# An encoder's residual, added by a DMA from GpSimd instead of a load and a VectorE addition

## The chip, the cores and the metric

The kernel runs on one core of a Trainium2 chip. The core has five engines that run side by side, each in its own fixed order of instructions: TensorE (PE, with its weight loads as PEld), VectorE (DVE), ScalarE (ACT), GpSimd (POOL) and SyncE (SP). They meet through semaphores: an instruction waits until another engine, or a DMA, has counted up. DMAs are started by an instruction on SP, ACT or POOL and then run on the core's 16 DMA engines.

The metric is the device time of one execution in microseconds (us), median over runs. Three runs of the kernel before took 2087.84, 2090.29 and 2091.57 us, so the median is 2090.29 us.

## The reference

A two-layer encoder over one sequence of 1024 tokens of width 1024, all in float32. Each layer is

```python
h = _rmsnorm(x, g_pre_mix[l])
z = h @ w_in[l]                       # split in Fourier, q, k, v and memory-query parts
y_f = _fourier_mix(zf, w_fourier[l])
y_a = _window_attn(q, k, v, sink[l])  # 8 query heads, window of 128
y_m = _memory_attn(zm, km, vm)
y = concat([_rmsnorm(y_f), _rmsnorm(y_a), _rmsnorm(y_m)]) @ w_out[l]
x = x + _rmsnorm(y, g_post_mix[l])    # the addition that the change moves

h = _rmsnorm(x, g_pre_ffn[l])
gate, up = split(h @ w_ffn_in[l])
f = (silu(gate) * up) @ w_ffn_out[l]
x = x + _rmsnorm(f, g_post_ffn[l])
```

with `_rmsnorm(y, g) = y * rsqrt(mean(y*y) + 1e-6) * g` over a row of 1024.

## The kernel before

**Tiles.** The 1024 tokens are 8 tiles (t = 0 to 7) of 128 partitions x 1024 floats. Float32 products are made from two float32r halves of each operand (`split`, L151 on ACT and L152 on DVE or POOL), three matmuls per product.

**The stage around the change.** Of the product with w_out, the Fourier and memory groups come first; their sum goes to DRAM (`pmd`). Then a loop over i (L1383 ff.) is skewed over the tiles: it does the attention of the second key/value head for tile i (`att_units`, scores sc, softmax scaling by POOL at L785, transposes pT, values av), the attention group's product with w_out for tile i-2 (`out`, matmuls `mo`), and the transposes of the finished rows of tile i-4 into the FFN's operand blocks (`Blocks.tile`, matmuls `hTp`, L1066). `Blocks.sum` and `Blocks.last` then form the sums and halves that the FFN's block products (a Strassen scheme, matmuls qx, qy, qz, qw, L1137) need.

**One tile's rows.** `out_rows` loads two tiles of rows by SP: f, the partial sum from `pmd` (L1027), and x, the residual from the input or, in the second layer, from the first layer's result `x2d` (L1028). `out` adds the matmul result to f (two DVE instructions at L1041). `residual` squares f with a row sum on ACT (L335), takes the reciprocal root on POOL (two instructions of one column, L210 and L212, names rrsv and rrs), scales f on DVE (L337) and adds it to x on DVE (L338). `norm_x` squares x on ACT (L289), stores x to `x1d` by an ACT DMA (L291), takes the root on POOL (nrsv, nrs) and scales x into f's place on DVE (L294). What lies in f then is the FFN's input, which PE transposes. The scale grs of the attention group is a POOL instruction too (L962), after the DVE instruction ms (L960).

**Places in SBUF.** x and f come from a ring of six places of 4 KB per partition (`xfs`, numbers 16, 20, 24, 28, 32, 0): tile 5 has x in 32 and f in 0, tile 6 has x in 16 and f in 20, tile 7 has 24 and 28. The first four weight loads of the FFN (two for the gate quad, two for the up quad, L1112) go to 32, 0, 16 and 20, so they wait until tiles 5 and 6 have left them.

**What sets the order.** The program is written as a list of operations, and a scheduler with its own model of times fixes the order on each engine, PE and SP included; at run time each engine keeps that order. A DVE addition that becomes a DMA is therefore also a cause for another order.

Of the kernel before, what the change touches and what calls it, by code (L numbers as in the profile page):

```python
# [16 lines left out]
ALU = mybir.AluOpType  # L17
# [3 lines left out]
D = 1024  # L21
S = 1024
NT = S // P
# [43 lines left out]

@with_exitstack
def tile_encoder(ctx: ExitStack, tc: tile.TileContext, T, C, out):
    nc = tc.nc  # L70

# [49 lines left out]
    def run(k, n, step):  # L121
        return Ring(*[k + i * step for i in range(n)])
# [6 lines left out]
    sqs, pms, xfs = run(16, 2, 2), run(20, 2, 2), Ring(16, 20, 24, 28, 32, 0)  # L129
# [8 lines left out]
    def sm(n, name="v"):  # L138
        if name not in smp:
            smp[name] = ctx.enter_context(tc.tile_pool(name="sm_" + name, bufs=N_SM.get(name, 4)))  # L140
        return smp[name].tile([P, n], F32, tag=name, name=nm(name))

    def ps(shape, name="ps", tag="pd"):
        return psp[tag].tile([P] + list(shape), F32, tag=tag, name=nm(name))
# [24 lines left out]
    def cst(*shape):  # L169
# [20 lines left out]
        out=mask[:, 0:P], in_=mask[:, 0:P], pattern=[[1, P]], compare_op=ALU.is_ge,  # L190
# [4 lines left out]
        out=mask[:, 2 * P : 3 * P], in_=mask[:, 2 * P : 3 * P], pattern=[[-1, P]],  # L195
# [11 lines left out]
    def rsqrt_mean(ss, n, width, name="rs"):  # L207

        v = sm(width, name + "v")
        nc.gpsimd.tensor_scalar(out=v, in0=ss, scalar1=1.0 / n, scalar2=EPS, op0=ALU.mult, op1=ALU.add)  # L210
        r = sm(width, name)
        nc.gpsimd.tensor_tensor(out=r, in0=v, in1=mhalf[:, 0:width], op=ALU.pow)  # L212
        return r
# [72 lines left out]
    def norm_x(x, g, h=None, keep=None):  # L286

        ss = sm(1, "nss")
        nc.scalar.activation(junks(D // 2).bitcast(BF16) if h is None else h, x, AF.Square, accum_out=ss)  # L289
        if keep is not None:  # L290
            nc.scalar.dma_start(keep, x)  # L291
        h = x if h is None else h
        r = rsqrt_mean(ss, D, 1, "nrs")
        nc.vector.scalar_tensor_tensor(out=h, in0=x, scalar=r[:, 0:1], in1=g, op0=ALU.mult, op1=ALU.mult)  # L294
        return h
# [32 lines left out]
            (nc.gpsimd if t in (1, 3) else nc.vector).tensor_tensor(out=x[:, ns], in0=x[:, ns], in1=f[:, ns], op=ALU.add)  # L328
            (nc.sync, nc.scalar)[n].dma_start(dst[:, ns], x[:, ns])

    def residual(x, f, g, eng=None):

        junk = junks(D // 2).bitcast(BF16)
        ss = sm(1, "rss")
        nc.scalar.activation(junk, f, AF.Square, accum_out=ss)  # L335
        r = rsqrt_mean(ss, D, 1, "rrs")
        nc.vector.scalar_tensor_tensor(out=f, in0=f, scalar=r[:, 0:1], in1=g, op0=ALU.mult, op1=ALU.mult)  # L337
        (eng or nc.vector).tensor_tensor(out=x, in0=x, in1=f, op=ALU.add)  # L338


    def scaled(raw, g, k):
# [144 lines left out]
    class Mix:  # L486
# [536 lines left out]
            self.prepped[t] = self.split_y(parts, yys), self.group_scale(parts, AW, sqs)  # L1023

        def out_rows(self, t, xsrc, pmd):
            self.xf[t] = x, f = xfs(D), xfs(D)
            nc.sync.dma_start(f, pmd)  # L1027
            nc.sync.dma_start(x, xsrc)  # L1028

        def out(self, t, x1):  # L1030

            x, f = self.xf.pop(t)
            (hi, lo), rs = self.prepped.pop(t)
            for n in range(2):
                ns = slice(n * 512, n * 512 + 512)
                pt = ps([512], "mo")
                acc = Acc(pt, 4)
                for i in range(4):
                    w = self.woa[2 + i]
                    acc.add(hi[:, i], lo[:, i], w[0][:, ns], w[1][:, ns])  # L1040
                nc.vector.scalar_tensor_tensor(  # L1041
                    out=f[:, ns], in0=pt, scalar=rs[:, 0:1], in1=f[:, ns], op0=ALU.mult, op1=ALU.add
                )
            residual(x, f, self.gpost)
            return norm_x(x, self.gffn, f, x1)


# [181 lines left out]
    def out_sums(l, actd, i, k):  # L1229
# [23 lines left out]
        return ab  # L1253

    def ffn_out(l, actd, load, out, after, half, late):


# [14 lines left out]
        for i in (5, 3, 4, 1, 7, 2, 6):  # L1272
# [5 lines left out]
            for k in range(n):  # L1278
                ops.append(out_sums(l, actd, i, k))
                for p in range(whole):  # L1280
                    step(pts[p], p, ops[k], k == 0, k == n - 1, new)
                t = {(2, 2): 0, (2, 7): 1, (6, 1): 2, (6, 5): 3}.get((i, k))
                if t is not None:
                    load(t)
                    out(t, rows[t])
                if i == 6 and k in (7, 8, 9, 10):
                    load(k - 3)
# [71 lines left out]
    for l in range(DEPTH):  # L1359
# [69 lines left out]
        def last_tile(t, f):  # L1429
            if t == 0:  # L1430
                st["gpf"] = gain(T["g_post_ffn"][l], at(8, D))
            x = xt.pop(t)
            if l == DEPTH - 1:
                residual_out(x, f, st["gpf"], x_out[t], t)
                return
            residual(x, f, st["gpf"], nc.gpsimd if t < 4 else None)
            nc.sync.dma_start(x2d[t], x)
            token_scale(x, t)
            st[t] = x
            if t:  # L1440
                norm_T(st.pop(t - 1), nhT, t - 1, "av")
# [62 lines left out]
```

## Time and profile before

| | |
|---|---|
| median of three runs (range) | 2090.29 us (2087.84 to 2091.57) |
| the profiled execution: span from its first to its last instruction | 2089.2 us |
| mean granted TensorE clock in it | 0.981 |
| PE busy | 1994.7 us (95%) |
| DVE busy | 1578.8 us (76%) |
| ACT busy | 1069.9 us (51%) |
| POOL busy | 713.1 us (34%) |

The page lists the span of the profiled execution and no separate time for it; the span lies 1.1 us under the median of the runs. The stage of the change runs from about 320 to 424 us in layer 0 and from about 1350 to 1450 us in layer 1. In the rows of a timeline the columns are start, duration, engine, line, operation, written tile<-read tiles, shape and count; in brackets the idle time before it and what ended that. In a table of windows each engine's column is its busy time with its count of instructions.

### The profile page before, as it was taken

How to read it: one execution, taken by the hardware profiler on the slowest of the kernel's cores; microseconds unless marked ns; L12 is line 12 of the kernel's file. 1: busy time of each engine (PE TensorE's matmuls, PEld its weight loads, DVE VectorE, ACT ScalarE, POOL GpSimd, SP SyncE). 2: the span in 40 equal slices, each digit the busy share in tenths (PEclk: the TensorE clock that was granted, in tenths of full speed). 3: DMA queues.
4: the chain of work that ended last, by engine and by line, in shares of the span. 5: the costliest groups of instructions: out<-in, count | busy, mean ns of one | idle time of the engine just before them, and what ended most of it. 6: DMA issues, size and time to landing. Idle time of an engine off the chain costs nothing.

```text
span 2089.2 us, 28535 instructions
## 1 busy us (share of the span) xinstructions
PE 1994.7 (95%) x9587; PEld 1646.5 (79%) x9587; DVE 1578.8 (76%) x2540; ACT 1069.9 (51%) x2270; POOL 713.1 (34%) x819
## 2 busy tenths in 40 slices
PE   7998999799999999999999979997999999989998
PEld 6876787578888888887788768775788888878886
DVE  5558767898787877778867686579878787778767
ACT  6467777654333333544555677675433333345441
POOL 4344435433333423002523544453343342320002
PEclk9999999999999999999999999998999999999999
DMA  6111132423232333879831122233233232269874
GB/s 211 51 51 61 56 112 91 162 71 101 97 120 87 126 96 116 312 271 328 279 133 45 48 66 86 77 134 118 86 104 114 86 131 96 92 210 343 303 261 151
DMA packets 173347, 286.48 MB, mean 137 GB/s; under 512 B 15464, under 2 KB 73360, under 8 KB 173200
## 3 DMA queue, kind: packets, MB, share of 16 engines
q1 hardware_dynamic: 165136, 265.78, 37.9%
q10 hardware_dynamic: 8064, 18.88, 2.3%
q8 instruction: 75, 1.23, 0.2%
q14 instruction: 72, 0.59, 0.1%
HBM read 218.02 MB, written 66.58 MB: 136 GB/s over the span
## 4 chain that ended last, share of the span: by engine, by line
PE 74%; DVE 9%; DMA 7%; ACT 5%; issue 3%; POOL 2%; SPq 0%; DVEq 0%; ACTq 0%; POOLq 0%
PE fo L1270 13%; PE qx L1137 11%; PE qy L1137 10%; PE qz L1137 10%; PE mo L162 7%; PE qw L1137 5%; PE kvp L162 4%; DVE arena_r L152 3%; PE qp L162 3%; DMA arena_f<-actd 3%; PE zT L162 2%; PE pT L798 1%; ACT arena_r L151 1%; DMA arena_f<-in_w_ffn_out 1%; PE sc L761 1%
## 5 line engine op out<-in xcount | busy, mean ns | idle before, releaser
L151 ACT CAST arena_r<-arena_f 128x512 fp32r<-128x512 f32 (+1 forms) x780 | 443.7, 591 | 632.6 <-PE qz L1137 119.9
L152 DVE TENSOR_TENSOR arena_r<-arena_f,arena_r 128x512 fp32r<-128x512 f32 (+1 forms) x676 | 509.4, 774 | 148.1 <-ACT arena_r L151 136.8
L1270 PE MATMUL fo<-arena_r 128*128 128x512 f32 x1848 | 425.1, 391 | 8.7 <-ACT arena_r L151 7.3
L1270 PEld LDWEIGHTS fo<-arena_r 128*128 128x128 f32 x1848 | 346.6, 188 | 82.4 <-ACT arena_r L151 8.1
L1137 PE MATMUL qy<-arena_r 128*128 128x512 f32 x1056 | 261.9, 397 | 22.3 <-ACT arena_r L151 12.5
L1137 PEld LDWEIGHTS qy<-arena_r 128*128 128x128 f32 x1056 | 201.7, 192 | 66.6 <-ACT arena_r L151 13.3
L1127 DVE TENSOR_TENSOR arena_f<-arena_f 128x512 f32<-128x512 f32 x220 | 205.9, 939 | 8.9 <-issue 2.4
L1137 PE MATMUL qz<-arena_r 128*128 128x512 f32 x704 | 196.6, 389 | 1.1 <-DVE arena_r L152 1.1
L1157 POOL TENSOR_TENSOR arena_f<-arena_f 128x512 f32<-128x512 f32 x44 | 73.9, 1679 | 310.2 <-ACT arena_f L1142 310.2
L1137 PEld LDWEIGHTS qz<-arena_r 128*128 128x128 f32 x704 | 132.1, 188 | 28.9 <-DVE arena_r L152 1.5
L152 POOL TENSOR_TENSOR arena_r<-arena_f,arena_r 128x256 fp32r<-128x256 f32 (+2 forms) x104 | 87.0, 842 | 129.5 <-ACT arena_r L151 84.4
L1137 PE MATMUL qx<-big,arena_r 128*128 128x512 f32 x528 | 127.1, 389 | 1.7 <-ACT arena_f L1142 1.7
L1137 PE MATMUL qx<-arena_r 128*128 128x512 f32 x528 | 127.9, 389 | 0.5 <-ACT arena_r L151 0.5
L1137 PE MATMUL qw<-arena_r 128*128 128x512 f32 x528 | 128.3, 389 | 0.0
L1189 POOL TENSOR_TENSOR arena_f<-arena_f 128x512 f32<-128x512 f32 x40 | 66.7, 1667 | 159.7 <-DVE arena_f L1169 122.4
L1137 PEld LDWEIGHTS qx<-big,arena_r 128*128 128x128 f32 x528 | 99.0, 188 | 22.6 <-ACT arena_f L1142 2.1
L1137 PEld LDWEIGHTS qx<-arena_r 128*128 128x128 f32 x528 | 99.1, 188 | 21.4 <-ACT arena_r L151 0.9
L1137 PE MATMUL qz<-big,arena_r 128*128 128x512 f32 x352 | 115.7, 389 | 0.0
L1137 PEld LDWEIGHTS qw<-arena_r 128*128 128x128 f32 x528 | 99.1, 188 | 20.6
L210 POOL TENSOR_SCALAR rrsv<-rss 128x1 f32<-128x1 f32 x32 | 13.6, 424 | 267.6 <-ACT arena_f L323 210.0
L162 PE MATMUL mo<-big,arena_r 128*128 128x512 f32 x384 | 102.2, 406 | 0.8 <-ACT arena_f L1001 0.8
L162 PE MATMUL mo<-arena_r 128*128 128x512 f32 x384 | 100.7, 403 | 0.9 <-POOL arena_r L152 0.6
(228 smaller groups left out, 3518.3 us busy)
## 6 DMA issues: line engine op xcount, KB each, us to landing
arena_f<-in_w_ffn_out SPq DMA_DIRECT2D x264, 256.0 KB, 4.6
arena_f<-in_w_ffn_in SPq DMA_DIRECT2D x88, 512.0 KB, 3.7
actd<-arena_f SPq DMA_DIRECT2D x154, 256.0 KB, 3.7
arena_f<-actd SPq DMA_DIRECT2D x154, 256.0 KB, 4.5
arena_f<-in_w_in SPq DMA_DIRECT2D x40, 256.0 KB, 3.0
arena_f<-in_x SPq DMA_DIRECT2D x16, 512.0 KB, 5.3
arena_f<-in_w_out SPq DMA_DIRECT2D x32, 256.0 KB, 2.7
pmd<-arena_f ACTq DMA_DIRECT2D x32, 256.0 KB, 2.0
```

The lines of the kernel that those rows point to most:

```text
L151: nc.scalar.copy(hi, src)
L152: return (lo_eng or nc.vector).tensor_tensor(out=lo, in0=src, in1=f32(hi), op=ALU.subtract)
L162: mm(self.dst, a, b, start=self.i == 0, stop=self.i == self.n - 1)
L210: nc.gpsimd.tensor_scalar(out=v, in0=ss, scalar1=1.0 / n, scalar2=EPS, op0=ALU.mult, op1=ALU.add)
L761: mm(pt, lhs, self.kst[g][i][:, k0 * P : k1 * P], start=i == 0, stop=i == 1)
L798: nc.tensor.transpose(pT[:, h, :], es_[h // 2][:, h % 2, j * P : j * P + P], ident)
L1127: nc.vector.tensor_tensor(out=s, in0=a, in1=b, op=op)
L1137: mm(pt, a, b, start=start and n == 0, stop=n == 11, skip_group_check=not start)
L1157: nc.gpsimd.tensor_tensor(out=self.v, in0=self.v, in1=self.s2, op=ALU.add)
L1189: (G if i in (0, 3) else V).tensor_tensor(out=a[i], in0=c, in1=g[i], op=ALU.mult)
L1270: mm(pt, ab[:, 0, x, sl], ab[:, 1, y], start=new and first and j == 0, stop=last and j == 2, skip_group_check=not new)
```

## The change

For tiles 0 to 6 the load of x into SBUF and the DVE addition are left out. In their place, once DVE has scaled f (L337), POOL issues a DMA that reads x's rows from DRAM and adds them to f in SBUF (L339 of the changed kernel). The sum therefore lies in f's place, not in x's, and x's place is only the target of the normed rows: the two names are exchanged. Tile 7 keeps the load and the addition on DVE, and so does the second residual of a layer (`residual` in `last_tile`).

```diff
-    def residual(x, f, g, eng=None):
+    def residual(x, f, g, eng=None, rows=None):
...
         nc.vector.scalar_tensor_tensor(out=f, in0=f, scalar=r[:, 0:1], in1=g, op0=ALU.mult, op1=ALU.mult)
-        (eng or nc.vector).tensor_tensor(out=x, in0=x, in1=f, op=ALU.add)
+        if rows is not None:
+            nc.gpsimd.dma_start(f, rows, accum_op=ALU.add)
+        else:
+            (eng or nc.vector).tensor_tensor(out=x, in0=x, in1=f, op=ALU.add)
...
         def out_rows(self, t, xsrc, pmd):
-            self.xf[t] = x, f = xfs(D), xfs(D)
+            x, f = xfs(D), xfs(D)
             nc.sync.dma_start(f, pmd)
-            nc.sync.dma_start(x, xsrc)
+            if t == NT - 1:
+                nc.sync.dma_start(x, xsrc)
+            self.xf[t] = x, f, xsrc if t < NT - 1 else None
...
         def out(self, t, x1):
-            x, f = self.xf.pop(t)
+            x, f, rows = self.xf.pop(t)
...
-            residual(x, f, self.gpost)
+            residual(x, f, self.gpost, rows=rows)
+            if rows is not None:
+                x, f = f, x
             return norm_x(x, self.gffn, f, x1)
```

The order of the instructions moves as well. The line numbers of the changed kernel are higher by 3 (up to `out_rows`) or 7 (behind `out`); the number behind a name only tells buffers apart.

POOL at the end of the stage in layer 0, before: the roots of tile 5 (rrs_3934, nrs_3943), of tile 6 (rrs_4025, nrs_4034), the halves of tile 7's attention rows (L152) and the scales grs of tiles 6 and 7.

```order
L212 TENSOR_TENSOR rrs_3934<-rrsv_3932,const 128x1
L962 TENSOR_TENSOR grs_3866<-ms_3864,const 128x1
L210 TENSOR_SCALAR nrsv_3941<-nss_3938 128x1
L212 TENSOR_TENSOR nrs_3943<-nrsv_3941,const 128x1
L210 TENSOR_SCALAR rrsv_4023<-rss_4021 128x1
L212 TENSOR_TENSOR rrs_4025<-rrsv_4023,const 128x1
L152 TENSOR_TENSOR arena_r<-arena_f,arena_r 128x256
L962 TENSOR_TENSOR grs_3991<-ms_3989,const 128x1
L210 TENSOR_SCALAR nrsv_4032<-nss_4029 128x1
L212 TENSOR_TENSOR nrs_4034<-nrsv_4032,const 128x1
```

The same place in the change, behind tile 5's first root (nrs_3937 is tile 5's second, rrs_4018 and nrs_4027 are tile 6's):

```order
L152 TENSOR_TENSOR arena_r<-arena_f,arena_r 128x256
L339 DMA arena_f<-in_x 128x1024
L965 TENSOR_TENSOR grs_3860<-ms_3858,const 128x1
L210 TENSOR_SCALAR rrsv_4016<-rss_4014 128x1
L212 TENSOR_TENSOR rrs_4018<-rrsv_4016,const 128x1
L210 TENSOR_SCALAR nrsv_3935<-nss_3932 128x1
L212 TENSOR_TENSOR nrs_3937<-nrsv_3935,const 128x1
L339 DMA arena_f<-in_x 128x1024
L152 TENSOR_TENSOR arena_r<-arena_f,arena_r 128x256
L965 TENSOR_TENSOR grs_3984<-ms_3982,const 128x1
L210 TENSOR_SCALAR nrsv_4025<-nss_4022 128x1
L212 TENSOR_TENSOR nrs_4027<-nrsv_4025,const 128x1
```

Each DMA waits for DVE's L337 of its tile. Tile 6's stands ahead of the halves of tile 7's rows, and the root of tile 5's second norm has moved behind tile 6's first.

POOL in the middle of the stage, tile 3 of layer 0, before (rrs_3668 is tile 3's root; L785 is the softmax scaling of a later tile):

```order
L212 TENSOR_TENSOR rrs_3668<-rrsv_3666,const 128x1
L785 TENSOR_SCALAR arena_f<-arena_f,rden_3630 128x384 x4
L152 TENSOR_TENSOR arena_r<-arena_f,arena_r 128x256 x2
L962 TENSOR_TENSOR grs_3600<-ms_3598,const 128x1
L210 TENSOR_SCALAR nrsv_3675<-nss_3672 128x1
L212 TENSOR_TENSOR nrs_3677<-nrsv_3675,const 128x1
L785 TENSOR_SCALAR arena_f<-arena_f,rden_3763 128x384 x4
```

and in the change (rrs_3664 is tile 3's):

```order
L212 TENSOR_TENSOR rrs_3664<-rrsv_3662,const 128x1
L152 TENSOR_TENSOR arena_r<-arena_f,arena_r 128x256
L339 DMA arena_f<-in_x 128x1024
L965 TENSOR_TENSOR grs_3596<-ms_3594,const 128x1
L788 TENSOR_SCALAR arena_f<-arena_f,rden_3758 128x384 x4
```

The DMA and the scale grs now stand ahead of a group of softmax scalings.

PE at the end of the stage in layer 0, before (hTp_4110 and hTp_4116 are the transposes of tile 5, hTp_4163 those of tile 6; mo_4066 and mo_4080 are tile 7's products; qy is the FFN's first product):

```order
L162 MATMUL mo_4080<-arena_r 128x512 x6
L1066 MATMUL hTp_4110<-const,arena_f 128x128 x4
L1066 MATMUL hTp_4116<-const,arena_f 128x128 x2
L162 MATMUL mo_4066<-arena_r 128x512 x2
L1066 MATMUL hTp_4116<-const,arena_f 128x128
L162 MATMUL mo_4080<-arena_r 128x512 x2
L1066 MATMUL hTp_4116<-const,arena_f 128x128
L958 MATMUL ssp_3984<-const,arena_f 128x2 x2
L162 MATMUL mo_4066<-arena_r 128x512 x4
L162 MATMUL mo_4080<-arena_r 128x512 x4
L1137 MATMUL qy_4136<-arena_r 128x512 x2
L1066 MATMUL hTp_4163<-const,arena_f 128x128 x4
```

and in the change (hTp_4103 and hTp_4109 are tile 5's, hTp_4156 tile 6's, mo_4059 and mo_4073 tile 7's):

```order
L162 MATMUL mo_4073<-arena_r 128x512 x6
L162 MATMUL mo_4059<-arena_r 128x512 x2
L162 MATMUL mo_4073<-arena_r 128x512 x2
L961 MATMUL ssp_3977<-const,arena_f 128x2 x2
L162 MATMUL mo_4059<-arena_r 128x512 x4
L162 MATMUL mo_4073<-arena_r 128x512 x4
L1073 MATMUL hTp_4103<-const,arena_f 128x128 x4
L1073 MATMUL hTp_4109<-const,arena_f 128x128 x4
L1144 MATMUL qy_4129<-arena_r 128x512 x2
L1073 MATMUL hTp_4156<-const,arena_f 128x128 x4
```

The transposes of tile 5 have moved behind all of tile 7's products. On SP the seven loads of x are gone from each layer's queue, and nothing else is added there.

## The prediction

> **What bounds the kernel now.** I began with the page's span and busy times, then read the stage of the change in a table of windows, and then followed its end instruction by instruction.
>
> ```profile
> span 2089.2 us, 28535 instructions
> PE 1994.7 (95%) x9587; PEld 1646.5 (79%) x9587; DVE 1578.8 (76%) x2540; ACT 1069.9 (51%) x2270; POOL 713.1 (34%) x819
> ```
>
> PE sets the time almost everywhere. DVE's share of 76% says nothing yet about what one DVE instruction is worth, so the stage is cut into its middle and its end, in both layers:
>
> ```profile
> core 0: us, PE busy (x) PEld busy (x) DVE busy (x) ACT busy (x) POOL busy (x), PEclk, DMA share, GB/s
> 340.00:380.00 40.00, 39.61 (x242) 31.20 (x241) 29.84 (x63) 31.51 (x83) 26.37 (x40) 1.00 0.39 138
> 380.00:420.00 40.00, 26.14 (x124) 20.10 (x122) 36.94 (x53) 22.51 (x43) 13.91 (x15) 0.87 0.53 176
> 1380.00:1420.00 40.00, 39.36 (x235) 30.92 (x234) 30.96 (x58) 31.82 (x79) 24.06 (x36) 1.00 0.45 158
> 1420.00:1445.00 25.00, 12.66 (x38) 9.06 (x38) 23.57 (x34) 12.71 (x23) 8.98 (x7) 0.66 0.45 148
> ```
>
> In the middle (rows 1 and 3) PE is full and DVE has a quarter free: a DVE addition less is worth nothing there, and anything that makes PE wait costs its full length. At the end (rows 2 and 4) PE stands for 13.9 and 12.3 us, and DVE is busy 92 to 94%. There a DVE instruction may count. What the end of layer 0 looks like on PE, ACT and SP:
>
> ```profile
> 390.23 0.82 PE L1066 MATMUL hTp<-const,arena_f 128*128 128x128 f32 x6
> 392.40 2.10 PE L162 MATMUL mo<-arena_r 128*128 128x512 f32 x8
> 399.76 1.22 PE L1137 MATMUL qy<-arena_r 128*128 128x512 f32 x2 [5.25 <-ACT arena_r L151]
> 403.35 1.97 PE L1066 MATMUL hTp<-const,arena_f 128*128 128x128 f32 x8 [2.38 <-DVE arena_f L294]
> 413.68 4.78 PE L1137 MATMUL qy<-arena_r 128*128 128x512 f32 x14 [5.56 <-ACT arena_f L1142]
> 396.26 0.62 ACT L151 CAST arena_r<-arena_f 128x512 fp32r<-128x512 f32 x1 [2.40 <-DMA arena_f<-in_w_ffn_in]
> 396.79 1.05 ACT L289 ACTIVATE arena_f<-arena_f 128x1024 f32<-128x1024 f32 x1
> 397.74 0.19 ACT L289 ACTIVATION_READ_ACCUMULATOR arena_f<-arena_f 128x1 f32 x1
> 410.45 0.62 ACT L151 CAST arena_r<-arena_f 128x512 fp32r<-128x512 f32 x1 [2.29 <-DMA arena_f<-in_w_ffn_in]
> 405.35 5.07 DMA arena_f<-in_w_ffn_in
> ```
>
> (The last row is from the chain of waits.) PE ends tile 7's products at 394.50, waits for the FFN's first weights, does two matmuls, waits for tile 6's rows, transposes them until 405.32, and this transposing frees the place of the last weight load: 5.07 us later ACT casts it (410.45), and only behind that cast, ACT being in order, comes the square of tile 7. So three things are late one after the other: the gate's weights, tile 6, the up quad's weights.
>
> **The change part by part.** *Removed on DVE:* 7 additions per layer, each
>
> ```profile
> L338 DVE TENSOR_TENSOR arena_f<-arena_f x16: 1211/1217/1641, 329.7 to 1435.1; 128x1024 f32<-128x1024 f32 x16
> 382.54 1.28 DVE L337 SCALAR_TENSOR_TENSOR arena_f<-arena_f,rrs 128x1024 f32<-128x1024 f32 x1
> 384.41 1.21 DVE L338 TENSOR_TENSOR arena_f<-arena_f 128x1024 f32<-128x1024 f32 x1
> 390.08 1.75 DVE L337 SCALAR_TENSOR_TENSOR arena_f<-arena_f,rrs 128x1024 f32<-128x1024 f32 x1 [0.44 <-POOL rrs L212]
> 394.16 1.21 DVE L338 TENSOR_TENSOR arena_f<-arena_f 128x1024 f32<-128x1024 f32 x1
> 402.02 1.28 DVE L294 SCALAR_TENSOR_TENSOR arena_f<-arena_f,nrs 128x1024 f32<-128x1024 f32 x1
> 1422.92 1.21 DVE L338 TENSOR_TENSOR arena_f<-arena_f 128x1024 f32<-128x1024 f32 x1
> ```
>
> 14 x 1.217 = 17.0 us of DVE. Tiles 0 to 4 have theirs under a full PE and are worth 0. Those of tiles 5 (384.41) and 6 (394.16) lie in the crowded end: at most 2 x 1.217 = 2.4 us per layer, if DVE's throughput decides it. Seven loads of x per layer fall away too, each 0.33 us of SP's time (row below); no row of this end waits for one of them, so they are worth 0.
>
> *Added:* a DMA that adds, issued by POOL behind L337. No row of the trace has such a transfer, nor any transfer issued by POOL. The nearest are plain loads of the same 512 KB, issued by SP:
>
> ```profile
> L1028 SPq DMA_DIRECT2D arena_f<-in_x x8: 328/330/385, 247.6 to 379.3; - x8
> DMA to landing us min/median/max: 3.3/3.7/5.3
> DMA to landing us min/median/max: 3.5/4.5/5.9
> ```
>
> (The second row belongs to L1028, the third to the FFN's weight loads, L1112, which run at the same time as the last two additions.) From below an adding transfer lands in 3.3 us. From above I double the slowest load, since f has to be read besides: 2 x 5.9 = 11.8 us. I take 6.0: the crowded median 4.5 and a third for the second read. The issue is bounded below by SP's 0.33 us, above by the longest that a tiny POOL instruction took in this end:
>
> ```profile
> 390.01 0.73 POOL L152 TENSOR_TENSOR arena_r<-arena_f,arena_r 128x256 fp32r<-128x256 f32 x1
> 396.12 3.94 POOL L962 TENSOR_TENSOR grs<-ms,const 128x1 f32<-128x1 f32 x1 [5.37 <-DVE ms L960]
> 400.14 0.19 POOL L210 TENSOR_SCALAR nrsv<-nss 128x1 f32<-128x1 f32 x1
> 400.42 0.55 POOL L212 TENSOR_TENSOR nrs<-nrsv,const 128x1 f32<-128x1 f32 x1
> 355.70 3.36 POOL L785 TENSOR_SCALAR arena_f<-arena_f,rden 128x384 f32<-128x384 f32 x4
> ```
>
> One column took 3.94 us at 396.12 and 0.55 at 400.42. I take 1.5 us for the issue, nearer to the quiet row, since most of the 14 are issued in the middle. The price so is 7.5 us from the end of L337 to the sum in place, between 3.6 and 15.7.
>
> The Trainium skill gives a price too: DMA: Bandwidth & Descriptors, section "Anatomy of one DMA — SWDGE (gpsimd) path", fits a POOL-issued DMA as 2.0 us plus its bytes at 436 GB/s, so 3.2 us here, as an estimate. By it tile 6's sum would be in place at 391.83 + 3.2 = 395.0 us instead of 399.3, and the end would go by the faster rival below; no row here shows such a transfer, and the page does not say that its fit holds for an adding one.
>
> *Tile 6, before:* L337 ends at 391.83, L338 starts 2.33 us later, behind four other DVE instructions, the sum is there at 395.37, ACT squares it at 396.79, the root ends at 400.97, held up by the grs of 3.94 us, L294 runs until 403.30. *After:* 391.83 + 7.5 = 399.3; square and read-out 1.24 us (1.05 and 0.19); two POOL instructions, 0.83 us (0.19 and 0.55 with the step between); L294 1.28 us: 402.7. That is 0.6 us earlier than before, because the old path had queues in it that the new one no longer meets. I count 0; at the bounds of 3.6 and 15.7 the end is 398.8 or 410.9, so -4.5 to +7.6.
>
> *Tile 5's transposes.* In the new order they follow all of tile 7's products, and they free place 32, where half of the gate's weights go. Tile 7's last eight products need the halves of L152, which now stands behind tile 6's DMA on POOL: 391.83 + 1.5 + 0.73 = 394.06 instead of 390.74, so the products run from 394.06 to 396.16, not 392.40 to 394.50. Then eight transposes, 1.0 us: 397.2. The load lands 4.5 us later, 401.7; from the cast at 396.26 to the first qy at 399.76 were 3.5 us: 405.2. Two qy, 1.2 us, and tile 6's transposes start at 406.4 instead of 403.35. This is +3.1 us for all that follows: the last weight load, ACT's cast and tile 7's square. DVE has work of its own in that gap and is relieved by 2.4 us; I let half of this, 1.2, come back. End of the stage: +1.9 us per layer, and the same for layer 1, whose PE stands in the same way; +3.8 in all. Bounds per layer: -2.4 (the transfer is quick and the reordering harmless) and +7.6.
>
> *What queues behind the DMA on POOL.* POOL is in order and now waits for L337. Behind some of the DMAs, with at most one instruction between, stand the four softmax scalings of a later tile (L785 before), as the second place of the order shows for tile 3. At 355.70 four scalings took 3.36 us, and PE reads the first soon after:
>
> ```profile
> 357.87 0.82 PE L798 MATMUL pT<-const,arena_f 128*128 128x128 f32 x6
> ```
>
> With the wait for L337 (1.28 us less the L152 of 0.73 that covers part of it) and the issue of 1.5, such a group starts about 2 us later. POOL's 13.6 free us in 340 to 380 are some 4 us per tile, so the load fits, but a late group makes PE wait, and PE is full. The pattern stands at 3 tiles in layer 0 and 5 in layer 1. For each I take 0.5 us of PE, between 0 (the order was made for it) and 2: +4.0 us, between 0 and 16.
>
> Sum: 2089.2 + 3.8 + 4.0 = 2097.0 us of span; the runs' median lies 1.1 above the span: 2098.1 us.
>
> **The rivals.** *Hidden on both sides (no change).* PE's queue was made for the new order, the scalings come in time, and at the end the 2.4 us that DVE gains meet the 3.1 us of the later weights: 2090 us. For it: tile 6 comes out within 0.6 us. Against: PE has no slack in the middle.
>
> *Faster: DVE decides the end.* The sum lands in under 4 us. Then L294 of tile 5 is no later than before, and DVE, 92 to 94% busy, ends its stage by its removed work earlier: 2 x 2.4 = 4.9 us, 2085.4. It decides from the point where the gate's weights arrive before DVE has split the operands. For it: DVE's short gaps in row 2, 3.1 us of 40. Against: the two longest stops of PE in the end are released by ACT, and ACT's casts wait for weight loads.
>
> *Slower by far: POOL's issue is starved.* In the end POOL's small instructions run several times their quiet time while DVE is full. If an issue takes 4 us instead of 1.5, each of the last two DMAs of a layer is 2.5 later, with the transfer crowded by weight loads towards 11.8: +7.6 per end. With the forecast's 4.0 for the middle this is 2090.3 + 15.2 + 4.0 = 2109.5; with half of the middle's bound, 8, it is 2113.5. For it: the 3.94 us row. Against: in the middle POOL's column instructions mostly take 0.55. The Trainium skill, SBUF — State Buffer, section "SBUF: two separate sides", has a rule that speaks for it: POOL writes the descriptors of its DMAs into SBUF by itself and cannot while DVE runs in a mode that takes the port pair which both share. The same page ("Who interferes with whom") says that DVE instructions with two SBUF inputs, which fill this end, hold up only POOL instructions that read SBUF, which would spare the issue; the stretched 128x1 rows agree with the second part, and no row here shows an issue by POOL.
>
> **How the numbers follow.** The forecast (slower by about 8 us) 37%, hidden 26%, faster 19%, starved 18%. The time is the forecast's, 2098.1. About 0.2%, 4.2 us, is what a measurement of this kernel can tell from no change; the runs above spread by 3.7. The forecast's own range is 2093 to 2104. The range that holds 8 in 10 reaches to the faster rival and to the starved one, 2085 to 2113. Of the forecast nearly all lies above 0.2%, of the faster rival nearly all below: faster 0.20, same 0.26, slower 0.54.
>
> **What would show it.** Right: 14 DMAs on POOL with landing times near 6 us; tile 5's transposes at PE some 5 us later behind tile 7's products, and the first qy of each FFN later than before against the start of the stage; PE idle in the middle in front of pT, released by ACT or POOL. Wrong: landing under 4 us or over 10; PE as full in the middle as before; the end shorter by DVE's 2.4 us. What would overturn it altogether is a difference outside this stage, since the order has changed in the FFN's first products and in layer 1's earlier stages too, and I count nothing for that.

## The result, and the profile after

The changed kernel takes 2106.41 us (median of four runs, 2103.10 to 2109.68) against 2090.93 us for the kernel before, measured with it (2087.84 to 2091.99): 1.0069 times as long, 95% interval 1.0051 to 1.0087. It is slower by 15.5 us, 0.7%. The forecast was 2098.1 with a range of 2085 to 2113: its sign was right, its size was half of what came, and the experiments below show that neither of its two terms made the time.

The profiled execution of the changed kernel is the longest of its four runs; its span is 18.7 us longer than that of before. The head of its page:

```profile
span 2107.9 us, 28539 instructions
PE 2007.7 (95%) x9587; PEld 1653.7 (78%) x9587; DVE 1562.2 (74%) x2526; ACT 1070.3 (51%) x2270; POOL 722.6 (34%) x833
```

DVE is relieved by 16.6 us (17.0 were counted), POOL has 9.5 us more. PE does the same 9587 matmuls.

To find where the time went, I cut both traces at the first and the last product with w_out (`mo`) and at the first and the last FFN product `qy`. The *middle* runs from the first to the last `mo`, the *end* from there to the first `qy`, the *FFN part* from the first to the last `qy`:

| us | middle, layer 0 / 1 | end, layer 0 / 1 | FFN part, layer 0 / 1 | sum |
|---|---|---|---|---|
| before | 185.9 / 187.3 | 5.3 / 7.4 | 426.7 / 427.3 | 1239.8 |
| after | 196.3 / 197.6 | 8.7 / 11.3 | 419.9 / 423.8 | 1257.6 |
| difference | +10.4 / +10.3 | +3.5 / +3.9 | -6.8 / -3.4 | +17.8 |

So the middle loses 20.7 us, the end 7.4, and the FFN part gives 10.3 back. The forecast had +4.0 for the middle, +3.8 for the end and nothing for the rest. Windows over the last part of the middle and the end of layer 0, first of before, then of after (columns as in the prediction):

```profile
320.00:394.50 74.50, 74.11 (x430) 57.19 (x428) 56.37 (x109) 55.30 (x139) 40.94 (x64) 1.00 0.37 131
394.50:399.76 5.26, 0.01 (x2) 0.01 (x1) 5.15 (x9) 2.79 (x5) 3.64 (x1) 0.97 0.42 159
```

```profile
320.00:403.66 83.66, 77.26 (x424) 57.88 (x423) 51.28 (x105) 53.62 (x136) 44.73 (x72) 0.99 0.48 127
403.66:412.38 8.72, 1.39 (x8) 1.15 (x7) 8.03 (x12) 6.36 (x12) 2.20 (x5) 0.70 0.88 283
```

Before, PE was busy for 74.11 of 74.50 us. After, it stands for 6.4 us of 83.66, and its 424 matmuls take 3.2 us more than the 430 before.

Part of that is the granted clock: over the last four us (400 to 404) it was 0.65, and tile 7's last eight products took 3.19 us there against 2.10 before. Over both middles PE stands 20.4 us against 8.7 and is busy 9.0 us longer; the granted clock was 0.98 and 1.00 in them before, 0.97 and 0.98 after, which is worth up to some 6 of these 9.0. What lowers it is not shown: it was 0.50 just behind two of PE's stops (1.55 us up to 400.46, 1.63 us up to 1413.67), and 1.00 behind another of 2.38 us. The rest of the 9.0 I did not trace.

What the engines wait for there (some of the waits between 320 and 420 us, of PE's those in the middle; total, times, longest), before and then after:

```profile
POOL nrsv L210 <- ACT arena_f L289: 10.3, 4, 7.9
ACT arena_f L289 <- DVE arena_f L338: 5.9, 3, 3.2
DVE arena_f L294 <- POOL nrs L212: 1.6, 3, 0.7
```

```profile
POOL nrsv L210 <- ACT arena_f L289: 19.8, 7, 7.3
ACT arena_f L289 <- DMA arena_f<-in_x: 17.7, 7, 5.1
DVE arena_f L294 <- POOL nrs L212: 10.7, 4, 4.1
PE mo L162 <- POOL arena_r L152: 1.9, 2, 1.6
PE pT L801 <- ACT big L1074: 1.1, 1, 1.1
PE ssp L961 <- ACT arena_f L958: 1.0, 1, 1.0
PE mo L162 <- ACT arena_r L151: 1.0, 1, 1.0
PE sc L764 <- DVE rmax L765: 0.9, 1, 0.9
PE pT L801 <- POOL arena_f L788: 0.4, 1, 0.4
```

ACT waits for each of the seven transfers at L289, the square of the sum: 17.7 us where it waited 5.9 for the addition. POOL waits for that square, and DVE for POOL's root. Behind these waits PE's own come from all sides. How they hang together shows best in layer 1, at PE's longest stop of that middle (ACT's and PE's timelines):

```profile
1383.33 1.06 ACT L289 ACTIVATE arena_f<-arena_f 128x1024 f32<-128x1024 f32 x1 [1.77 <-DMA arena_f<-x2d]
1384.39 0.35 ACT L818 COPY arena_f<-av 128x256 f32<-128x256 f32 x1
1384.88 0.30 PE L801 MATMUL pT<-const,arena_f 128*128 128x128 f32 x1 [2.38 <-ACT arena_f L818]
```

ACT waits for the sum, squares it, and only then makes the copy for which PE stands 2.38 us. The prediction asked what stands behind the DMA on POOL, and never what stands behind the square on ACT. ACT's queue in the changed kernel at tiles 0 and 2, with DVE's instruction for the first (one timeline per engine):

```profile
332.89 1.06 ACT L806 COPY big<-pT 128x512 f32<-128x512 f32 x2
336.06 1.06 ACT L289 ACTIVATE arena_f<-arena_f 128x1024 f32<-128x1024 f32 x1 [2.10 <-DMA arena_f<-in_x]
337.11 0.60 ACT L777 ACTIVATE arena_f<-arena_f,nmx 128x384 f32<-128x384 f32 x1
...
355.70 1.06 ACT L289 ACTIVATE arena_f<-arena_f 128x1024 f32<-128x1024 f32 x1 [3.15 <-DMA arena_f<-in_x]
356.75 0.40 ACT L958 ACTIVATE arena_f<-arena_f 128x256 f32<-128x256 f32 x1
357.06 0.60 ACT L777 ACTIVATE arena_f<-arena_f,nmx 128x384 f32<-128x384 f32 x1
```

```profile
339.08 1.28 DVE L294 SCALAR_TENSOR_TENSOR arena_f<-arena_f,nrs 128x1024 f32<-128x1024 f32 x1 [2.61 <-POOL nrs L212]
```

The softmax exponentials (L777) of the attention tiles stand behind the squares. Before, the same two groups began 2.4 and 5.8 us earlier:

```profile
334.73 0.64 ACT L774 ACTIVATE arena_f<-arena_f,nmx 128x384 f32<-128x384 f32 x1
351.24 0.60 ACT L774 ACTIVATE arena_f<-arena_f,nmx 128x384 f32<-128x384 f32 x1
```

The DMA itself (the group of its line; its durations in ns are those of the issue on POOL):

```profile
L339 POOL DMA_DIRECT2D arena_f<-in_x x7: 900/911/1050, 330.4 to 398.7; - x7
L339 POOL DMA_DIRECT2D arena_f<-x2d x7: 902/912/929, 1364.9 to 1443.3; - x7
  ACT arena_f L289: 30.8, 13
DMA to landing us min/median/max: 5.3/5.6/8.2
```

The issue takes 0.91 us, the sum is there 5.6 us after the issue begins, and ACT waited 13 of 14 times, 30.8 us in all.

### The profile page after: what moved, and what is told of

Its sections match the earlier page's. It is cut to its first block, busy times and chain, and to the rows that moved or that the text cites. A ratio compares the mean times of both kernels' runs of the same rounds, so it can differ in the third digit from the quotient of the medians.

```text
span 2107.9 us, 28539 instructions
## 1 busy us (share of the span) xinstructions
PE 2007.7 (95%) x9587; PEld 1653.7 (78%) x9587; DVE 1562.2 (74%) x2526; ACT 1070.3 (51%) x2270; POOL 722.6 (34%) x833
## 4 chain that ended last, share of the span: by engine, by line
PE 79%; DMA 6%; DVE 5%; ACT 4%; POOL 3%; issue 2%; SPq 0%; DVEq 0%; POOLq 0%; ACTq 0%
PE fo L1277 17%; PE qx L1144 11%; PE qz L1144 11%; PE qy L1144 11%; PE mo L162 6%; PE qw L1144 6%; PE kvp L162 4%; PE qp L162 3%; PE zT L162 2%; PE pT L801 2%; DMA arena_f<-in_x 2%; DVE arena_r L152 1%; DMA arena_f<-actd 1%; DMA arena_f<-x2d 1%; PE sc L764 1%
## 5 line engine op out<-in xcount | busy, mean ns | idle before, releaser
L152 DVE TENSOR_TENSOR arena_r<-arena_f,arena_r 128x512 fp32r<-128x512 f32 (+1 forms) x676 | 509.3, 775 | 147.8 <-ACT arena_r L151 139.7
L1144 PE MATMUL qy<-arena_r 128*128 128x512 f32 x1056 | 262.4, 397 | 23.0 <-ACT arena_r L151 17.8
L152 POOL TENSOR_TENSOR arena_r<-arena_f,arena_r 128x256 fp32r<-128x256 f32 (+2 forms) x104 | 87.3, 849 | 120.6 <-ACT arena_r L151 88.8
```

What stands on the lines that cost most here:

```text
L152: return (lo_eng or nc.vector).tensor_tensor(out=lo, in0=src, in1=f32(hi), op=ALU.subtract)
L1144: mm(pt, a, b, start=start and n == 0, stop=n == 11, skip_group_check=not start)
```

## Experiments

The theories are *latency* (ACT squares the sum in order, waits for the transfer, and keeps what stands behind it from PE), *order* (the new sequence at the end of the stage, tile 5's transposes above all) and *POOL's queue* (its waits for L337 and its issues), the last two being the terms of the forecast. Each new order also moves instructions elsewhere, and single traces differ from their medians by some us, so verdicts go by the medians and their ratios, and the parts of the table by several traces together.

**1. The DMA for tiles 0 to 4 alone.**

```diff
-            if t == NT - 1:
+            by_dma = t < 5
+            if not by_dma:
                 nc.sync.dma_start(x, xsrc)
-            self.xf[t] = x, f, xsrc if t < NT - 1 else None
+            self.xf[t] = x, f, xsrc if by_dma else None
```

> The adding DMA for tiles 0 to 4 of each layer alone; tiles 5 to 7 keep the load of x and the VectorE addition. Three theories stand. Latency: ACT squares each sum (L289) in order and waits for the transfer (some 5.6 us from its issue, against 1.2 us for the addition), and what stands behind that square on ACT, and behind L294 on DVE, comes late to PE. In the changed kernel the last product of tile 7 ended 9.2 us later than before in layer 0 and 10.3 us later against the start of the mixing product in layer 1, so the middle holds most of the 15.5 us: 2099 to 2105 here, with ACT waiting for the DMA at L289 about 2 us per tile. Order: what costs is that tile 5's transposes follow tile 7's products; with tile 5 on DVE that is mostly undone, so 2090 to 2094. POOL's queue: POOL waits for L337 and issues, and softmax scalings stand behind it: 2094 to 2099 (my forecast's 4.0 us and its half as much again), with PE idle before pT released by POOL.

Measured: 2100.35 us, 1.0051 (1.0035 to 1.0067). This is the latency theory's range, above POOL's and order's. Two thirds of the loss are in the first five tiles; the middle is 14.7 us longer than before in the two layers together. PE's waits for pT behind POOL were 0.4 us in this stage of layer 0. But, against my expectation, the order was not undone: tile 5's transposes stand behind all of tile 7's products in layer 1 and behind all but one in layer 0. So run 1 alone does not tell latency from order.

**2. The DMA for tiles 5 and 6 alone** (the same edit with `t in (5, 6)`).

> The reverse: the adding DMA for tiles 5 and 6 of each layer alone. PE's order at the end of the stage is that of the changed kernel: tile 5's transposes behind all of tile 7's products. Latency: the middle is free of it, only the end pays; from the last product of tile 7 to the first FFN product the changed kernel took 3.4 us more than before in layer 0 and 4 us in layer 1, so 2092 to 2099. Order: all of the loss is here, 2098 to 2106. POOL's queue: no softmax scaling stands behind these two DMAs, so 2089 to 2093.

Measured: 2092.80 us, 1.0013 (1.0001 to 1.0024). At most a small loss, as latency had it; order, at 2098 or more, missed. POOL's range holds it too. PE has the new order here in layer 0 alone (in layer 1 tile 5's transposes stand ahead of tile 7's last twelve products), so what speaks against order is above all run 3, which has it in both layers.

**3. The new order of tile 5's transposes without the DMA**, in the kernel before: PE's instructions in `hb.tile` of tile 5 are queued behind the last product of tile 7 (`last_mo`).

```diff
...
-            if i >= 4:
-                hb.tile(hs.pop(i - 4), i - 4)
+            if i == 9:
+                with tc.issue_after(mix.last_mo.ins):
+                    hb.tile(hs.pop(i - 4), i - 4)
+            elif i >= 4:
+                hb.tile(hs.pop(i - 4), i - 4)
```

> The kernel before, with its load and VectorE addition for every tile, but tile 5's transposes are held on PE behind the last product of tile 7, as in the changed kernel; there is no adding DMA. Order: the gate's first weights come later, as my forecast has it, by 3.1 us per layer less what DVE gives back, so 2094 to 2099. Latency: the order alone is worth little, 2089 to 2093.

Measured: 2086.98 us, 0.9983 (0.9970 to 0.9996), below both ranges. This order alone costs nothing; it rather gains. What the forecast foresaw does happen locally, in the waits of PE around the end of layer 0:

```profile
PE qy L1138 <- ACT arena_r L151: 8.2, 1, 8.2
PE hTp L1067 <- DVE arena_f L294: 3.7, 1, 3.7
PE qy L1138 <- ACT arena_f L1143: 3.1, 1, 3.1
```

The first FFN product waits 8.2 us instead of 5.3, as far as foreseen. But that delay does not reach the end of the kernel (see below).

**4. The same DMA, for which nobody waits.** `spare` is DRAM that nobody reads.

```diff
...
-            nc.gpsimd.dma_start(f, rows, accum_op=ALU.add)
+            nc.gpsimd.dma_start(spare[nsp[0]], f, accum_op=ALU.add)
+            nsp[0] += 1
```

> The changed kernel, with the same DMA in the same place of the program, of the same size and with the same wait for L337, but it adds f to a spare place in DRAM that nobody reads. x is thereby left out of the first residual, so the result is another; no x is loaded, nothing waits for the transfer. POOL's issue, its wait for L337 and the transfer's traffic stay; only the latency is gone. Latency: 2086 to 2092, with no wait of ACT at L289 for a DMA. POOL's queue or traffic: 2098 to 2107, as slow as the changed kernel. The first FFN product should then be within 3 us of its time before, or 8 to 12 us late.

Measured: 2085.54 us, 0.9982 (0.9967 to 0.9998): 20.9 us less than the changed kernel. The group of its line (L342), as above:

```profile
L342 POOL DMA_DIRECT2D spare<-arena_f x14: 895/907/1054, 324.9 to 1415.7; - x14
  DVE arena_f L340: 10.8, 7
DMA to landing us min/median/max: 5.5/6.4/7.9
```

Fourteen issues of 0.91 us, POOL idle behind DVE's L340 (the L337 of the changed kernel) for 10.8 us, transfers even longer, and no loss. POOL's issues and the transfers' traffic are therefore not the cause; the wait for the landing is, or the order that comes with it. For the scheduler gave other places here: tile 5's transposes stand ahead of tile 7's last products in both layers, and in layer 0 tile 6's DMA stands behind the halves of tile 7's rows. Runs 3 and 8 tell the two apart. (The time is 0.5 us under the range.)

**5. The addition left out altogether** (`pass` in place of the DMA).

> The changed kernel without the DMAs: no x is loaded or added for tiles 0 to 6, so x is left out of the first residual and the result is another. What remains is the relief of VectorE and SP. All theories put it at or below the unwaited DMA's 2085.5; the difference between the two is the price of POOL's 14 issues, its waits for L337 and the traffic: 0 to 2 us by the latency theory (2083 to 2086), 4 us or more by that of POOL's queue (2081 or less).

Measured: 2087.91 us, 0.9983 (0.9972 to 0.9995). I expected it at or below run 4; it lies 2.4 us above in its median, with nearly the same ratio. POOL's 14 issues and waits have no price that these runs can tell from zero.

**6. Half the bytes.**

```diff
-            nc.gpsimd.dma_start(f, rows, accum_op=ALU.add)
+            nc.gpsimd.dma_start(f[:, 0 : D // 2], rows[:, 0 : D // 2], accum_op=ALU.add)
```

> The changed kernel, where each DMA adds only the first 512 of 1024 columns; x is thereby left out of the other half of the first residual, so the result is another. The number of DMAs, their issue, POOL's waits and ACT's waits are as in the changed kernel; only the bytes of each are halved. From the unwaited DMA (2085.5) to the changed kernel (2106.4) lie 21 us for a latency of 5.6 us from issue to landing. Latency by bytes: landing near 4 to 4.5 us and a time of 2097 to 2102. Latency that is nearly all fixed: landing over 5 us, 2103 to 2108. Were it the traffic of the transfers rather than the waiting, the unwaited DMA, which moved as much, would have shown it, so under 2095 is not expected by any theory.

Measured: 2091.18 us, 1.0003 (0.9991 to 1.0015).

```profile
  ACT arena_f L289: 22.5, 13
DMA to landing us min/median/max: 3.8/4.1/6.4
```

The landing came as expected, 4.1 us, the time did not: with 1.5 us less of latency nearly all of the loss was gone, where I had expected a third of it, though ACT still waited 22.5 us. So the loss does not go in proportion to the latency or to ACT's waits; two points do not show the shape of the curve. The order is not the changed kernel's either: in layer 0 tile 5's transposes stand ahead of all of tile 7's products. There PE waits in the middle instead of the end (195.2 us and 0.3, against 196.3 and 8.7 in the changed kernel); in layer 1, which has the changed kernel's order, it is 187.4 and 10.4.

**7. The addition on POOL, for tiles 0 to 6.**

```diff
-            residual(x, f, self.gpost)
+            residual(x, f, self.gpost, nc.gpsimd if t < NT - 1 else None)
```

> The kernel before, with the addition of tiles 0 to 6 done by POOL in place of VectorE; the loads of x stay. A POOL addition of this size took 2.73 us (median) in the other residual of layer 0, so the sum is 1.5 us later than by VectorE instead of some 5, and VectorE is relieved of the same 17 us as by the change. Latency: a small part of the change's loss, if any, 2087 to 2094. If what counts is POOL being busy or waiting for L337 in its order (19 us more work per layer than none, against 6.4 us of DMA issues in the changed kernel): 2098 to 2106. If VectorE's relief is worth something that the latency hides: under 2087.

Measured: 2092.88 us, 1.0008 (0.9996 to 1.0020), the latency theory's range. A POOL that is busy for 2.39 us per tile in this place costs less than one that issues for 0.91 us and leaves the sum late.

**8. The changed kernel, with the square put later in ACT's queue.** `out` now hands back the second norm, and the loop issues its ACT instructions behind the next tile's L335 (`mix.square`):

```diff
...
-                hs[i - 2] = mix.out(i - 2, x1d[i - 2])
+                norms[i - 2] = mix.out(i - 2, x1d[i - 2])
+                if 1 <= i - 2 <= 5:
+                    with tc.issue_after(mix.square.ins):
+                        hs[i - 3] = norms.pop(i - 3)()
+                if i - 2 >= 5:
+                    hs[i - 2] = norms.pop(i - 2)()
```

> The changed kernel, with one thing moved: the second norm of tiles 0 to 4 is issued on ACT behind the square of the next tile's residual (L335 of tile t+1), so that ACT does other work while the sum is on its way. The same DMAs are issued behind the same L337. Latency through ACT's order: at least half of the middle's loss (9.2 and 10.3 us of 15.5) comes back, 2094 to 2101, and ACT waits for the DMA at L289 in fewer of tiles 0 to 4, for less than 10 us in a layer's stage instead of 17.7. If it is not ACT's order but the later rows themselves (the FFN's operands come late whatever stands behind them), the time stays: 2104 to 2110.

Measured: 2092.41 us, 1.0006 (0.9994 to 1.0018): 14.0 us less than the changed kernel with the same 14 DMAs. That is more than expected. PE's order at the end of the stage is that of the changed kernel in both layers; on POOL, in layer 0, tile 6's DMA stands behind the halves of tile 7's rows. The windows of layer 0 and the waits there:

```profile
320.00:393.14 73.14, 72.77 (x424) 57.27 (x423) 46.03 (x99) 52.63 (x135) 43.41 (x70) 1.00 0.51 137
393.14:404.70 11.56, 0.88 (x10) 0.64 (x7) 10.64 (x18) 6.85 (x13) 3.40 (x5) 0.64 0.67 182
```

```profile
DVE arena_f L294 <- POOL nrs L212: 6.9, 5, 2.5
ACT arena_f L289 <- DMA arena_f<-in_x: 5.0, 4, 2.1
```

```profile
DMA to landing us min/median/max: 5.3/5.6/7.7
```

The landing is the same 5.6 us. ACT's wait has fallen from 17.7 to 5.0 us, and PE is full again: as many matmuls as in the changed kernel, 424, take 72.77 us in 73.14, not 77.26 in 83.66. The end, 11.6 us, is even longer than in the changed kernel.

**9. The control: the kernel before with the square put later** (the loop of run 8, no DMA).

> The control of the moved norm: the kernel before, with its load and VectorE addition, and the second norm of tiles 0 to 4 issued on ACT behind the square of the next tile's residual, as in the kernel that took 2092.4 with the DMAs. If that move helped because it hides the transfer's latency, it has nothing to hide here and is worth little: 2088 to 2095. If it is simply a better order, it should gain here too what it gained there, 14 us: 2074 to 2080.

Measured: 2090.08 us, 0.9997 (0.9982 to 1.0011). The move is worth nothing where there is no latency to hide. With runs 3, 4 and 8 this speaks for one cause: the transfer's latency, sitting in ACT's order in front of other work. (PE's order moved here too: in both layers tile 5's transposes stand ahead of tile 7's products.)

**10 and 11. A version that beats both.** Run 8 with the DMA for tiles 0 to 4 alone (the edit of run 1), and then with tile 5's transposes held as in run 3 besides.

> The moved norm together with the adding DMA for tiles 0 to 4 alone; tiles 5 to 7 keep the load and the VectorE addition. Against tiles 0 to 4 without the move (2100.4) the move should take back most of the middle's loss; against the move with the DMA for tiles 0 to 6 (2092.4) the end is spared two transfers, which alone cost 2.1 us: 2087 to 2093. If VectorE's relief of 10 additions under a full TensorE is worth nothing, not below 2087.

> The same (moved norm, adding DMA for tiles 0 to 4), and tile 5's transposes held behind tile 7's last product, an order that took 2087.0 against 2090.7 with no DMA at all. If the two add up, this is the best of all: 2083 to 2089. If not, within 2 us of the kernel without the hold.

Measured: 2086.60 us, 0.9974 (0.9958 to 0.9990), and 2083.74 us, 0.9974 (0.9962 to 0.9986). Both are faster than the kernel before, and by far than the changed one; the hold adds nothing that the ratios can tell. Run 10 also repeats run 8 without a DMA for tile 6: against run 1, with the same ten DMAs, the later square is worth 13.8 us. The waits of the second in layer 0:

```profile
ACT arena_f L289 <- DMA arena_f<-in_x: 2.5, 2, 2.2
```

**12. The addition on POOL for tiles 0 to 4 alone** (the edit of run 7 with `t < 5`).

> The kernel before, with the addition on POOL for tiles 0 to 4 alone, in place of VectorE. The addition on POOL for tiles 0 to 6 took 2092.9, and its rows are 2.39 us, 1.2 longer than VectorE's, which a tile of the crowded end feels (mo's end to the first qy took 11.4 and 9.7 us there against 5.3 and 7.4 before). Without tiles 5 and 6: 2088 to 2092. Below 2087 would mean that VectorE's relief in the middle is worth something after all.

Measured: 2093.83 us, 1.0021 (1.0007 to 1.0035), a miss: I had expected it to be at or under run 7, and it is not faster. Its middle in layer 1 was 194.7 us long, 8.3 longer than in run 7, while layer 0 was alike. That is another order again: in layer 1 tile 5's transposes stand ahead of all of tile 7's products, PE waits 2.5 us for tile 5's rows there (DVE's L294), and the granted clock of that middle is 0.97 against 0.99. The end is shorter by more (none against 9.7 us), but the FFN part behind it is 6.3 longer.

## Why the prediction was right and wrong

The parts of the traces, both layers added, with the medians' difference to the kernel before in the same comparison:

| us | middle | end | FFN part | end + FFN part | median against before |
|---|---|---|---|---|---|
| before | 373.2 | 12.6 | 854.0 | 866.6 | |
| after | 393.8 | 20.0 | 843.7 | 863.8 | +15.5 |
| 1: DMA for tiles 0 to 4 | 387.8 | 17.3 | 846.7 | 864.0 | +9.7 |
| 2: DMA for tiles 5 and 6 | 373.8 | 18.1 | 851.2 | 869.2 | +2.2 |
| 3: order alone | 373.8 | 18.2 | 847.3 | 865.5 | -3.7 |
| 4: nobody waits | 374.7 | 7.6 | 853.5 | 861.1 | -5.1 |
| 5: left out | 373.1 | 1.7 | 863.5 | 865.3 | -3.2 |
| 6: half the bytes | 382.6 | 10.7 | 853.2 | 864.0 | +0.1 |
| 7: POOL adds, tiles 0 to 6 | 373.3 | 21.1 | 848.2 | 869.3 | +1.8 |
| 8: square later | 368.6 | 24.8 | 847.7 | 872.5 | +1.3 |
| 9: square later, no DMA | 375.4 | 7.7 | 861.0 | 868.7 | -0.9 |
| 10: 8 for tiles 0 to 4 | 368.0 | 17.6 | 851.7 | 869.3 | -4.4 |
| 11: 10 and the hold | 368.1 | 17.9 | 849.9 | 867.9 | -7.2 |
| 12: POOL adds, tiles 0 to 4 | 381.6 | 8.9 | 856.8 | 865.7 | +2.8 |

The end ranges over 23 us, but the end and the FFN part together stay within 861 and 873: where the first FFN product starts late, the stage behind it is shorter by nearly as much. PE's waits from just before the first `qy` to 480 us in layer 0 show it, before and then after:

```profile
PE qy L1137 <- ACT arena_f L1142: 5.6, 1, 5.6
PE qy L1137 <- ACT arena_r L151: 5.3, 1, 5.3
PE hTp L1066 <- DVE arena_f L294: 2.4, 1, 2.4
```

```profile
PE qy L1144 <- ACT arena_r L151: 7.3, 1, 7.3
PE qy L1144 <- ACT arena_f L1149: 1.1, 1, 1.1
```

Behind the longer first wait, the second falls from 5.6 to 1.1 us and that for tile 6's rows is gone. The middle is what is left. It is longest in the changed kernel, next in run 1, and in the other runs but 6 and 12 it is at most 2.2 us above its length before, or below it. Runs 6 and 12 are long in one middle each and take nearly the time of before: in these two layers tile 5's transposes stand ahead of all of tile 7's products, and PE stands in the middle instead of at the end, which takes 0.3 us and none.

The granted clock is not the cause. It was 0.976 to 0.981 in the four runs of the changed kernel and 0.975 to 0.984 in 35 of the kernel before; at 0.981 the changed kernel took 2103.10 us, more than any of these 35 (2083.20 to 2098.19).

By the prediction's steps:

- *What bounds the kernel.* Right for the middle: PE has no slack there, and what makes it wait is paid. Wrong for the end: I took its three late things as a chain whose delay the kernel pays, and it is largely given back.
- *The removed additions, worth 0 in the middle and up to 2.4 us per layer at the end.* Runs 4 and 5 gain 5.1 and 3.2 us without the latency, about the bound of 4.9. But run 3 gains 3.7 with every addition in place, so these runs do not show that it is DVE's relief. Run 10 is 3.5 us under its control, run 9, with ten additions gone from the middle: there "worth 0" may have been too low, but the intervals of the two ratios overlap.
- *The price of the DMA, 7.5 us (1.5 for the issue, 6.0 for the landing).* Mis-sized, but within its bounds: 5.6 us from the start of the issue, of which 0.91 is the issue. By the Trainium skill (DMA: Bandwidth & Descriptors, "Anatomy of one DMA — SWDGE (gpsimd) path") it would, as an estimate, have been 3.2 us; the adding DMA took 5.6, and with half its bytes 4.1. By these two points, as an estimate, the fixed part is 2.6 us and the 512 KB are worth 3.0, against 2.0 and 1.2 by that fit; the measurement decides.
- *Where that price is paid.* This is the step that failed. I followed it along tile 6's own path, where it came out 0.6 us earlier than before, and for the other tiles asked only what it delays on POOL, the engine that issues it. The instruction that waits for it is ACT's square at L289, in tiles 0 to 4 too: it stands in front of softmax exponentials, casts and copies that PE needs. Those waits, 17.7 us in the stage of layer 0, go with 10.4 us more of its middle; the forecast had no term for them. Run 8 brings the wait down to 5.0 us and the middle back to 185.0, as before.
- *POOL's scalings behind the DMA, +4.0 us.* Wrong: run 4, with as many issues and scalings in POOL's queue (in a partly different order), loses nothing, run 8 nearly nothing, and PE waited for the scalings 1.5 us in the whole trace of the changed kernel, against 0.7 before (who waited for L788 after, then for L785 before). The bound below, 0, was the right end.

```profile
  PE pT L801: 1.5, 3
```

```profile
  PE pT L798: 0.7, 1
```

- *Tile 5's transposes behind tile 7's products, +1.9 us per layer.* The mechanism was there (the first `qy` waits 3 us more in run 3), the price was not: in the sum it is zero or a gain. The halves of tile 7's rows behind tile 6's DMA did hold up PE, by 1.55 us in layer 0 of the changed kernel:

```profile
398.74 0.91 POOL L339 DMA_DIRECT2D arena_f<-in_x  x1
399.39 1.02 POOL L152 TENSOR_TENSOR arena_r<-arena_f,arena_r 128x256 fp32r<-128x256 f32 x1
400.46 3.19 PE L162 MATMUL mo<-arena_r 128*128 128x512 f32 x8 [1.55 <-POOL arena_r L152]
```

- *Tile 6 counted at 0.* Not separable in the after trace, where its L337 itself comes later. Run 2, tiles 5 and 6 together, is 2.2 us slower, so 0 was close.
- *Nothing for the rest of the kernel.* Wrong by the 10.3 us that the FFN part gave back; the prediction named this as what could overturn it.
- *The rivals.* A starved issue gave nearly the right time (2109.5) for a wrong reason: the 14 issues took 0.90 to 1.05 us, those at the crowded end (390 and 399 us) as those in the middle. The Trainium skill's rule that DVE can keep POOL from writing descriptors (SBUF — State Buffer, "SBUF: two separate sides") did not come to bear; that DVE instructions with two SBUF inputs spare it (same page, "Who interferes with whom") agrees with these rows. The faster rival needed a sum in under 4 us; it took 5.6. The hidden one expected the scalings in time, which they nearly were, and like the forecast it had nothing for ACT's square.

So the forecast was slower by 7.8 us from two terms of which neither holds, and the 15.5 us that came are a third one, of 20.7 us in the middle, less what the end and the FFN part together gave back. That the sign was right, and the time inside the range, was luck. What stays open is how the loss depends on the latency, and how much of the lower clock in the middle goes with the waits.

## What to carry to other kernels

When an operation is replaced by a slower one that runs elsewhere, find the instruction that waits for its result, and list what stands behind it on its in-order engine; the engine that issues the transfer may be the harmless one. If the latency can't be shortened, move the waiting instruction back in its queue: the same transfers then cost almost nothing here. A delay just in front of a stage that itself waits for loads is mostly given back, one in a full stage is hardly given back, so price the two apart.

## What had not been expected of the hardware

An adding DMA of 512 KB, issued by POOL, occupies POOL for 0.91 us and lands 5.6 us after its issue begins, against 3.7 us for the plain load of the same rows issued by SP; with 256 KB it lands in 4.1 us. The same number of bytes, added from SBUF into DRAM, lands in 6.4 us. The issue was not longer where DVE was busy: it took 0.89 to 1.06 us over all runs with 512 KB. On POOL the 128x1024 addition took 2.39 us against 1.22 on DVE, and 2.73 in the other residual of the kernel before.
